# A hybrid decoder trunk on one core: the first stage in a written order with four column groups, the convolution's shifted copies by DMA, and a bias added as matrix products

## The chip, the cores and the metric

The kernel runs on one core of one Trainium2 chip. The core has five engines with instruction streams of their own: TensorE (PE, with its weight loads shown apart as PEld), VectorE (DVE), ScalarE (ACT), GpSimd (POOL) and SyncE (SP). Sixteen DMA engines move data between the chip's memory and the core's SBUF. The metric is the device time of one execution in microseconds (us).

## The reference

Two layers over 256 tokens with D = 2048 features, all in float32. Layer 0 mixes tokens with a Conformer convolution module, layer 1 with differential attention; each is followed by an MLP with 8192 hidden units. Every sublayer is modulated by vectors computed from one condition vector c (adaLN). What matters here is layer 0:

```python
cond = silu(c)
mod = cond @ ada_w[i] + ada_b[i]                # 2048 x 12288 weights per layer
sh_m, sc_m, g_m, sh_f, sc_f, g_f = split(mod, 6)
h = x * (1.0 + sc_m) + sh_m
# conformer_conv
u = h @ w1 + b1                                 # pw1: 2048 x 4096
a, gt = split(u, 2)
u = a * sigmoid(gt)
u = causal_depthwise_conv(u, w_dw, width=31) + b_dw
u = silu(layer_norm(u, g, b))
y = u @ w2 + b2                                 # pw2: 2048 x 2048
x = layer_norm(ALPHA * x + g_m * y)
h = x * (1.0 + sc_f) + sh_f                     # then the MLP, gated by g_f
```

## The kernel before

**Products.** TensorE multiplies in a fast 32-bit format with a rounded mantissa, so each float32 operand is split into a high and a low part. ACT casts a weight tile to the high part (`CAST wh...`, line 424), DVE subtracts it from the original (`wl...`, line 426), and each 128x128 by 128x512 step takes three products: high times high (L440), high times low weights (L441), low times high (L442). The 256 tokens are two row tiles t = 0, 1. KC = 16 chunks of 128 features are summed. pw1 is cut into eight column groups j of 256 value and 256 gate columns; a group of 16 chunks is 16 x 2 x 3 = 96 products in two PSUM banks. A weight tile of 4 chunks is 1 MB, loaded by two DMAs of 512 KB on SP's queue (L417) into one of four `wraw` buffers.

**Modulation vectors.** Each of the six vectors of a layer needs 16 MB of `ada_w`, read as 1 MB tiles `aw` (L206). DVE can do a tile: multiply by cond and add into `aacc` (L236), followed at the end by products with ones that sum over partitions (`apt`, L218). Or TensorE can: `aps` products with cond as 32 columns, eight per tile (L268), a copy by ACT to a row (L272), and transposes back (L253). In the first stage ada tiles and weight tiles share the four `wraw` buffers, and two `araw` buffers serve ada tiles alone.

**First stage.** `SLICES` cuts the 16 chunks into four slices of four. For each slice SC_M comes by DVE, SH_M by TensorE; h is formed transposed (`h_t`, split into `h_hi` and `h_lo`); and three groups of pw1, `FIRST = (2, 0, 1)`, add the slice's products. They stay open in PSUM over the four slices. The order on all engines is left to the scheduler of the tile framework. The stage ends with the last slice's products, at 188 us.

**Groups 3 to 7 and the convolution.** Then TensorE's order is as written. Each of the other five groups runs through its 16 chunks (`group`). `tick()` after every second chunk runs steps that were deferred with `defer(n, step)`. A finished group is copied from PSUM (`utok`, L760), transposed (L773, L774), and gated by ACT and DVE to u (L781, L783). The convolution (`conv_pe`) is done by TensorE on 32 features at a time: the 31 taps are eight products of four shifts each. For that u is laid out in four shifted copies, by 16 copies of 32 partitions per group, 12 by ACT (L729) and 4 by DVE (L731); then 64 products with 32 columns for each of two 128-feature halves (L738). Tap matrices are made by DVE (`conv_w`, L720).

**Other ada tiles.** G_M, SC_F and SH_F are needed later: `pump_conv` issues them beside the groups, `fill` in the tail behind the last group, `pump_t2` the rest during pw2. SH_F is done by TensorE, the others by DVE. By the start of pw2 42 of these 48 tiles are issued.

**Gate and bias.** `gate_and_base` (at tick 28) spreads the gate G_M to all partitions through two dependent DMAs (`gb_d`, `gb`), and `base_bias` loads the bias of pw2, multiplies it by the gate and adds it to z, all on POOL (L659, L663). pw2 runs from 420.6 us on in four column groups (L526 to L528); the gated result is added to z by DVE.

Of the kernel before, what the change touches and what calls it, by code (L numbers as in the profile page):

```python
# [19 lines left out]
P = 128  # L20
# [10 lines left out]
FIRST = (2, 0, 1)  # L31
ADA_T1 = 32
# [17 lines left out]
CV_AT = (1, 4)  # L50
OV_AT = (2, 4)
# [5 lines left out]
MAN_AT = None  # L57
SC_PE = ()
SLICES = ((0, 4), (4, 4), (8, 4), (12, 4))
SHIFT = ("act", "act", "act", "dve")  # L60
SHIFT_END = ("act", "dve", "act", "dve")
CONV_AT = {2: 1, 0: 4, 1: 7}
PE_WAIT = (3, 4)
# [16 lines left out]
def trunk(  # L80
# [114 lines left out]
    n_raw = [0]  # L195

# [13 lines left out]
    def ada_slice_dve_steps(i, v, f0, nf, m, first=True):  # L210
# [14 lines left out]
        def step(a):  # L225
            wv = load(a)
# [11 lines left out]
            if kc == KC - 1:  # L238
                if first:
                    finish()  # L240
                else:
                    defer(DVE_WAIT, finish)
        return [lambda a=a: step(a) for a in range(KC // per)]

    def ada_slice_steps(i, v, f0, nf, m, first=False, apart=False):
# [16 lines left out]
        def step(a):  # L262
            wv = st.pop(a, None) or load(a)
# [6 lines left out]
            if kc == KC - 1:  # L270
                st["rows"] = work.tile([P, NG], F32, tag="A", name=f"arow_{i}_{v}_{f0}")[:, :w]
                nc.scalar.copy(st["rows"], st["ps"])  # L272
                if first:
                    finish()
                else:
                    defer(2, finish)
        steps = [lambda a=a: step(a) for a in range(KC // per)]
        if apart:
            return [lambda a=a: st.update({a: load(a)}) for a in range(KC // per)], steps
# [41 lines left out]
    ada_q = []  # L321
    m_gm, m_scf, m_shf = mod_tile(0, G_M), mod_tile(0, SC_F), mod_tile(0, SH_F)
    for f0 in (0, 8):
        ada_q.extend(ada_slice_dve_steps(0, G_M, f0, 8, m_gm, False))
# [15 lines left out]
    n_late = 7 * KC  # L340

    def pump_early(n):
        for _ in range(n):
            if len(ada_q) > n_late:
                ada_q.pop(0)()
# [24 lines left out]
    def to_featT(src, pair, mul, add, name, c2s=None):  # L370

        for c2 in (range(KC // 2) if c2s is None else c2s):
            pt = tp_tile(f"{name}_t{c2}")
            for j in range(2):
                cc = 2 * c2 + j
                for t in range(NT):
                    nc.tensor.transpose(out=pt[:, j * S + t * P: j * S + (t + 1) * P],
                                        in_=src[:, t, cc * P:(cc + 1) * P], identity=ident)
            h32 = work.tile([P, 2, S], F32, tag="B", name=f"{name}_h{c2}")
            for j in range(2):  # L380
                cc = 2 * c2 + j
                if j == 0:
                    nc.vector.tensor_scalar(h32[:, j, :], pt[:, j * S:(j + 1) * S],
                                            mul[:, cc:cc + 1], add[:, cc:cc + 1], ALU.mult, ALU.add)
                else:
                    nc.scalar.activation(h32[:, j, :], pt[:, j * S:(j + 1) * S], AF.Identity,
                                         scale=mul[:, cc:cc + 1], bias=add[:, cc:cc + 1])
            put_split(pair, 2 * c2, 2, 0, S, h32)
# [24 lines left out]
    def load_split(src, name, on_pool=()):  # L413
        raw = wraw.tile([P, 2048], F32, tag="raw", name=f"w_{name}")[:, :src.shape[1] * NG]
        rv = raw.rearrange("p (a h n) -> p a h n", a=src.shape[1], h=src.shape[2])
        for h in range(src.shape[2]):
            raws["dma"] = nc.sync.dma_start(rv[:, :, h, :], src[:, :, h, :])  # L417
        parts = []
        per = 1024 // NG
        for q in range(src.shape[1] // per):  # L420
# [4 lines left out]
            eng = nc.gpsimd if q in on_pool else nc.vector  # L425
            eng.tensor_tensor(lo, rq, hi.bitcast(F32), op=ALU.subtract)  # L426
# [5 lines left out]
    def mm_parts(pss, pair, parts, kc0, nk):  # L432

        hi, lo = pair
        for a, (wh, wl) in enumerate(parts):
            kc = kc0 + a
            for t in range(NT):
                xh = hi[:, kc, t * P:(t + 1) * P]
                xl = lo[:, kc, t * P:(t + 1) * P]
                nc.tensor.matmul(pss[t], lhsT=xh, rhs=wh, start=(kc == 0), stop=False)  # L440
                nc.tensor.matmul(pss[t], lhsT=xh, rhs=wl, start=False, stop=False)  # L441
                nc.tensor.matmul(pss[t], lhsT=xl, rhs=wh, start=False, stop=(kc == nk - 1))  # L442
            if a % 2:
                tick()

    def group(pair, srcs, name, pump, on_pool=()):
# [4 lines left out]
        for i, src in enumerate(srcs):  # L451
            parts = load_split(src, f"{name}_{i}", on_pool)
            pump()
            mm_parts(pss, pair, parts, kc, nk)
# [8 lines left out]
    def add_group(key, pair, srcs, lead=False, tail=False, pump=None, start=None, pre_t=None, on_t=None,  # L463
                  only=None, prep=None, between=None, on_pool=()):
# [6 lines left out]
        for blk in blocks:  # L471
            if only is not None and blk[0] not in only:
# [3 lines left out]
                             start=start if first else None, pre_t=pre_t if first else None, pre_done=False, prep=prep if first else None, on_t=on_t,  # L476
# [25 lines left out]
    def run_jobs():  # L502
        banks, h = {}, 0
        for n, job in enumerate(jobs):
# [9 lines left out]
            def half(j, t):  # L514
# [3 lines left out]
                for a, (wh, wl) in enumerate(split[h + j]):  # L518
                    kc = kc0 + a
                    for tt in t:  # L520
# [5 lines left out]
                        nc.tensor.matmul(pss[tt], lhsT=xh, rhs=wh, start=(kc == 0), stop=False)  # L526
# [165 lines left out]
    XW = UW - 3  # L692
    ux = big.tile([P, 4096], F32, tag="uTh", name="conv_ux")
    xs_buf = [ux[:, 0:8 * XW], econv.tile([P, 8 * XW], F32, name="conv_x")]
    xs_buf = [x_.rearrange("p (n b s) -> p n b s", n=2, b=4) for x_ in xs_buf]
    u_buf = [ux[:, 8 * XW + i * 2 * UW:8 * XW + (i + 1) * 2 * UW].rearrange("p (n s) -> p n s", n=2) for i in range(3)]
# [15 lines left out]
    def conv_pe(j, u):  # L712


        xs = xs_buf[1 if j not in FIRST else FIRST.index(j) % 2]
        dg = [[], []]
# [8 lines left out]
        for b in range(4):  # L725
            for r in range(4):
                dst, src = xs[32 * r:32 * r + 32, :, b, :], u[32 * b:32 * b + 32, :, r:r + XW]
                if (SHIFT_END if j == 7 else SHIFT)[(r - b) % 4] == "act":
                    nc.scalar.copy(dst, src)  # L729
                else:  # L730
                    nc.vector.tensor_copy(dst, src)  # L731

        def products(n):
            ch = 2 * j + n
            ps = tp_tile(f"cv_{ch}")
            for k4 in range(8):
                for b in range(4):
                    nc.tensor.matmul(ps[32 * b:32 * b + 32, :S], lhsT=dg[n][k4 // 4][:, (k4 % 4) * 4 + b, :],  # L738
                                     rhs=xs[:, n, b, 4 * k4:4 * k4 + S],
                                     start=(k4 == 0), stop=(k4 == 7))  # L740
            dst = work.tile([P, S], F32, tag="S", name=f"vpe_{ch}", bufs=3)
            nc.scalar.activation(dst, ps[:, :S], AF.Identity, bias=cv["dwb"][:, ch:ch + 1])
            conv_done(ch, dst)
        return products

    n_conv = [0]
    n_early = len(ada_q) - n_late

    def pump_conv():
        n_conv[0] += 1  # L750
        while n_early - (len(ada_q) - n_late) < ADA_T1 * n_conv[0] / (4 * (8 - len(FIRST))):
            pump_early(1)

    conv_last = []

    def glu(j, pss, wait=1):
        ut = []
        for t in range(NT):
            u_t = work.tile([P, NG], F32, tag="A", name=f"utok_{j}_{t}")
            nc.scalar.copy(u_t, pss[t])  # L760
            ut.append(u_t)
        if j in FIRST:
            u = u_buf[FIRST.index(j)]
        else:
            u = work.tile([P, 2, UW], F32, tag="X", name=f"u_{j}", bufs=3)

        def rest():
# [630 lines left out]
```

## Time and profile before

| | us |
|---|---|
| median of 3 runs | 2434.58 (2431.07 to 2436.49) |
| profiled execution | 2432.41 |
| its span | 2430.6 |
| first stage ends (last product of the first three groups) | 188 |
| last product of pw1 | 386 |
| start of pw2 | 420.6 |
| first 128x512 products of the MLP's part behind pw2's | from about 514 on |

The span is the time between the first and the last instruction of the profiled execution; 1.8 us lie around it. The remaining 1900 us are the first MLP, the attention layer and the second MLP. In the profile's rows a name such as `L440 PE MATMUL pw_ps<-wh_pw,h_hi` reads: line 440 of the kernel, on PE, written tile, then the tiles read. A waits row names the waiting engine and tile, what ended the wait, then us in total, times, and the longest one.

### The profile page before, as it was taken

The numbers are of one execution on the slowest core, as the hardware profiler recorded it, in microseconds if no ns is written. First come the engines' busy times: TensorE is split into PE (matmuls) and PEld (weight loads), VectorE is DVE, ScalarE is ACT, GpSimd is POOL, SyncE is SP. The second block draws the span as 40 slices with busy tenths as digits, with TensorE's granted clock in tenths as the row PEclk, the third lists the DMA queues.
The fourth block names the chain that finished last, engine by engine and source line by source line (L and its number), as shares of the span: only waits on it lengthen the run. The fifth ranks groups of instructions, "written<-read, shape, count | busy, mean of one in ns | idle before, by whom it ended". The sixth has DMA issues, their size and how long they took to land.

```text
span 2430.6 us, 28467 instructions
## 1 busy us (share of the span) xinstructions
PE 2277.4 (94%) x11119; PEld 1816.0 (75%) x11119; DVE 1759.5 (72%) x1977; ACT 1070.6 (44%) x1391; POOL 264.9 (11%) x174
## 2 busy tenths in 40 slices
PE   4588997989999999999998999998999999999997
PEld 2366664867778888888876888886788888888886
DVE  5588744879798888878868777886867565565566
ACT  2337554444434434434444544443543443443442
POOL 0000011232150000000024200012214000000002
PEclk9789998999999999999999999999999999999999
DMA  9998767658988888888875666685676555556562
GB/s 354 312 331 292 247 220 263 240 209 290 333 309 319 293 322 278 315 314 294 299 254 189 203 237 220 236 291 185 236 277 227 190 186 190 191 185 197 181 223 102
DMA packets 272547, 609.57 MB, mean 251 GB/s; under 512 B 11098, under 2 KB 44448, under 8 KB 259100
## 3 DMA queue, kind: packets, MB, share of 16 engines
q1 hardware_dynamic: 271560, 607.24, 72.2%
q8 instruction: 87, 1.43, 0.2%
q10 hardware_dynamic: 852, 0.51, 0.1%
q14 instruction: 48, 0.39, 0.0%
HBM read 605.58 MB, written 2.13 MB: 250 GB/s over the span
## 4 chain that ended last, share of the span: by engine, by line
PE 75%; DVE 10%; DMA 6%; ACT 4%; issue 3%; POOL 1%; ACTq 0%; DVEq 0%; SPq 0%; POOLq 0%
PE w_ps L527 17%; PE w_ps L526 17%; PE w_ps L528 17%; DMA aw<-in_ada_w_dram 4%; DVE wl_w L494 2%; DVE aacc L236 2%; PE aps L268 1%; PE pw_ps L440 1%; DVE acc L294 1%; PE pw_ps L441 1%; PE qkv_q_ps L528 1%; PE pw_ps L442 1%; PE qkv_v_ps L528 1%; PE qkv_v_ps L526 1%; PE qkv_v_ps L527 1%
## 5 line engine op out<-in xcount | busy, mean ns | idle before, releaser
L494 DVE TENSOR_TENSOR wl_w<-w_w,wh_w 128x1024 fp32r<-128x1024 f32 x502 | 634.3, 1281 | 332.7 <-ACT wh_w L493 332.5
L493 ACT CAST wh_w<-w_w 128x1024 fp32r<-128x1024 f32 x512 | 537.5, 1053 | 754.1 <-PE w_ps L528 579.3
L526 PE MATMUL w_ps<-wh_w,hm_hi 128*128 128x512 f32 x1024 | 403.9, 394 | 4.5 <-ACT hm_hi L361 4.5
L527 PE MATMUL w_ps<-wl_w,u_hi 128*128 128x512 f32 x1024 | 399.0, 390 | 6.3 <-DVE wl_w L494 6.3
L527 PE MATMUL w_ps<-wl_w,hm_hi 128*128 128x512 f32 x1024 | 400.5, 391 | 4.7 <-DVE wl_w L494 4.7
L528 PE MATMUL w_ps<-wh_w,hm_lo 128*128 128x512 f32 x1024 | 400.8, 391 | 1.0 <-DVE hm_lo L364 1.0
L526 PE MATMUL w_ps<-wh_w,u_hi 128*128 128x512 f32 x1024 | 400.0, 391 | 0.0
L528 PE MATMUL w_ps<-wh_w,u_lo 128*128 128x512 f32 x1024 | 398.6, 389 | 0.0
L294 DVE SCALAR_TENSOR_TENSOR acc<-adaw,cond,acc 128x2048 f32<-128x2048 f32 (+1 forms) x105 | 243.0, 2315 | 0.1
L526 PEld LDWEIGHTS w_ps<-wh_w,hm_hi 128*128 128x128 f32 x1024 | 193.2, 189 | 49.2 <-ACT hm_hi L361 6.2
L527 PEld LDWEIGHTS w_ps<-wl_w,u_hi 128*128 128x128 f32 x1024 | 192.3, 188 | 47.9 <-DVE wl_w L494 8.4
L527 PEld LDWEIGHTS w_ps<-wl_w,hm_hi 128*128 128x128 f32 x1024 | 193.5, 189 | 45.1 <-DVE wl_w L494 6.0
L528 PEld LDWEIGHTS w_ps<-wh_w,hm_lo 128*128 128x128 f32 x1024 | 193.2, 189 | 43.0 <-DVE hm_lo L364 2.6
L526 PEld LDWEIGHTS w_ps<-wh_w,u_hi 128*128 128x128 f32 x1024 | 192.3, 188 | 42.0 <-issue 2.5
L528 PEld LDWEIGHTS w_ps<-wh_w,u_lo 128*128 128x128 f32 x1024 | 192.2, 188 | 39.9
L494 POOL TENSOR_TENSOR wl_w<-w_w,wh_w 128x1024 fp32r<-128x1024 f32 x10 | 24.0, 2404 | 1095.7 <-ACT wh_w L493 1095.7
L236 DVE SCALAR_TENSOR_TENSOR aacc<-aw,cond,aacc 128x512 f32<-128x512 f32 (+1 forms) x120 | 128.2, 1069 | 16.0 <-DMA aw<-in_ada_w_dram 14.0
L426 DVE TENSOR_TENSOR wl_pw<-w_pw,wh_pw 128x1024 fp32r<-128x1024 f32 x64 | 79.8, 1260 | 60.5 <-ACT wh_pw L424 60.4
L440 PE MATMUL pw_ps<-wh_pw,h_hi 128*128 128x512 f32 x256 | 106.6, 416 | 6.2 <-ACT h_hi L361 6.2
L441 PE MATMUL pw_ps<-wl_pw,h_hi 128*128 128x512 f32 x256 | 102.7, 401 | 0.0
L442 PE MATMUL pw_ps<-wh_pw,h_lo 128*128 128x512 f32 x256 | 99.1, 396 | 0.0
L424 ACT CAST wh_pw<-w_pw 128x1024 fp32r<-128x1024 f32 x64 | 65.9, 1048 | 68.6 <-PE pw_ps L442 58.7
(322 smaller groups left out, 3189.4 us busy)
## 6 DMA issues: line engine op xcount, KB each, us to landing
w_w<-in_mlp_w_dram SPq DMA_DIRECT2D x256, 1024.0 KB, 5.5
adaw<-in_ada_w_dram SPq DMA_DIRECT2D x96, 1024.0 KB, 6.1
aw<-in_ada_w_dram SPq DMA_DIRECT2D x84, 1024.0 KB, 7.3
w_pw<-in_conv_pw_w_dram SPq DMA_DIRECT2D x64, 512.0 KB, 7.2
w_pw<-in_conv_pw_w_dram SPq DMA_DIRECT2D x16, 1024.0 KB, 5.2
w_qkv_q<-in_attn_qkv_w_dram SPq DMA_DIRECT2D x16, 1024.0 KB, 5.3
w_qkv_k<-in_attn_qkv_w_dram SPq DMA_DIRECT2D x16, 1024.0 KB, 5.1
w_qkv_v<-in_attn_qkv_w_dram SPq DMA_DIRECT2D x16, 1024.0 KB, 5.2
```

What stands on the lines that cost most here:

```text
L236: nc.vector.scalar_tensor_tensor(st["acc"], wv[:, kc % per, :], cond[:, kc:kc + 1], st["acc"], ALU.mult, ALU.add)
L294: nc.vector.scalar_tensor_tensor(st["acc"], w, cond[:, kc:kc + 1], st["acc"], ALU.mult, ALU.add)
L424: nc.scalar.copy(hi, rq)
L426: eng.tensor_tensor(lo, rq, hi.bitcast(F32), op=ALU.subtract)
L440: nc.tensor.matmul(pss[t], lhsT=xh, rhs=wh, start=(kc == 0), stop=False)
L441: nc.tensor.matmul(pss[t], lhsT=xh, rhs=wl, start=False, stop=False)
L442: nc.tensor.matmul(pss[t], lhsT=xl, rhs=wh, start=False, stop=(kc == nk - 1))
L493: nc.scalar.copy(hi, rq)
L494: eng.tensor_tensor(lo, rq, hi.bitcast(F32), op=ALU.subtract)
L526: nc.tensor.matmul(pss[tt], lhsT=xh, rhs=wh, start=(kc == 0), stop=False)
L527: nc.tensor.matmul(pss[tt], lhsT=xh, rhs=wl, start=False, stop=False)
L528: nc.tensor.matmul(pss[tt], lhsT=xl, rhs=wh, start=False, stop=(kc == nk - 1))
```

## The change

1. **First stage.** The slices become (0,2), (2,4), (6,4), (10,4), (14,2), as first chunk and count. Four groups take part instead of three: `RES = (0, 1)` stay in PSUM; `ROT = (2, 3)` are closed after each slice and summed in SBUF, by an ACT copy for the first slice and a DVE addition for the others, in parts of `vtok`. PE, DVE, ACT and SP follow the order written in the code. Ada tiles no longer share `wraw`: they use two `araw` buffers and two halves of the tile `ux` (`conv_ux`), so four ada and four weight tiles can be in flight. The end of a slice's modulation (`end_ada`) stands in the middle of the previous slice's last group. The loads of `other_vectors` (nine small ones on ACT's queue) stand behind slice 2.
2. **Convolution.** `conv_pe` is cut into `conv_shift`, `conv_taps` and `conv_products`, placed at ticks `CONV_AT`. The shifted copies of groups 0 to 6 become 16 DMAs each on ACT's queue, of 32 partitions x 571 floats (73 KB); group 7 keeps copies, 8 by ACT and 8 by DVE. Two 128-feature halves are one copy with the padding between them.
3. **Ada tiles.** There are two queues: `dve_q` (16 tiles of G_M, 8 of SC_F) and `pe_q` (16 of SH_F, and 8 of SC_F that DVE did before). Twenty `dve_q` tiles run beside groups 4 to 7, eight `pe_q` tiles in the tail, and the remaining 16 of `pe_q` and 4 of `dve_q` during pw2.
4. **Bias and gate.** The bias of pw2 is added by two products (high and low part) that open each PSUM bank, with a one-row selector as stationary operand: 16 products. `base_bias` is not called for this layer any more. The gate's broadcast moves from tick 28 to the tail, behind the last convolution products.
5. The copies that fill `wct` are fewer and larger.

```diff
-FIRST = (2, 0, 1)
-ADA_T1 = 32
+RES = (0, 1)
+ROT = (2, 3)
+SLICES = ((0, 2), (2, 4), (6, 4), (10, 4), (14, 2))
+ADA_T1 = 20
-CONV_AT = {2: 1, 0: 4, 1: 7}
+CONV_AT = (3, 7, 11, 15, 19, 23, 28)
...
     def ada_raw(name, first):
-        n_raw[0] += 1
-        if first and n_raw[0] % 3:
-            return wraw.tile([P, 2048], F32, tag="raw", name=name)
+        if first:
+            n_raw[0] += 1
+            if n_raw[0] % 4 in (3, 0):
+                return ux[:, n_raw[0] % 4 // 3 * 2048:(n_raw[0] % 4 // 3 + 1) * 2048]
         return araw.tile([P, 2048], F32, tag="araw", name=name)
...
-    ada_q.extend(ada_slice_dve_steps(0, SC_F, 0, 8, m_scf, False))
+    dve_q.extend(ada_slice_dve_steps(0, SC_F, 0, 8, m_scf, False))
     for f0 in range(0, KC, 4):
-        ada_q.extend(ada_slice_steps(0, SH_F, f0, 4, m_shf))
-    ada_q.extend(ada_slice_dve_steps(0, SC_F, 8, 8, m_scf, False))
+        pe_q.extend(ada_slice_steps(0, SH_F, f0, 4, m_shf))
+    for f0 in range(8, KC, 4):
+        pe_q.extend(ada_slice_steps(0, SC_F, f0, 4, m_scf))
...
+    def conv_shift(j):
+        u = cs[j]["u"].rearrange("p n s -> p (n s)")
+        for b in range(4):
+            for r in range(4):
+                dst, src = xs_buf[j % 2][32 * r:32 * r + 32, b, :XW], u[32 * b:32 * b + 32, r:r + XW]
+                if j < 7:
+                    nc.scalar.dma_start(dst, src)
+                elif (r - b) % 2:
+                    nc.vector.tensor_copy(dst, src)
+                else:
+                    nc.scalar.copy(dst, src)
...
     for s, (f0, nf) in enumerate(SLICES):
         last = f0 + nf == KC
+        nxt = [] if last else ada_step[s + 1]
+        for n, g in enumerate(order[s]):
+            split_w()
+            pss = pss0[g] if g in RES else [tp_tile(f"pw1_{g}_{s}_ps{t}") for t in range(NT)]
+            k0, k1 = (0, KC - 1) if g in RES else (f0, f0 + nf - 1)
+            parts = w_parts.pop(0)
+            if n == len(order[s]) - 1 and not last:
+                mm_parts(pss, hT, parts[:nf // 2], f0, k0, k1, False)
+                end_ada(s + 1)
+                mm_parts(pss, hT, parts[nf // 2:], f0 + nf // 2, k0, k1, False)
+            else:
+                mm_parts(pss, hT, parts, f0, k0, k1, False)
+                for _ in range(2 if n == 0 and len(nxt) > 2 else 1):
+                    if nxt:
+                        ada_pair(s + 1)
+            if g in ROT:
+                for t in range(NT):
+                    if s == 0:
+                        nc.scalar.copy(accs[g][t], pss[t])
+                    else:
+                        nc.vector.tensor_tensor(accs[g][t], accs[g][t], pss[t], op=ALU.add)
+                cs[g]["ut"] = accs[g]
+            elif last:
+                glu_copy(g, pss)
+            if last and n in (1, 2):
+                glu(RES[n - 1])
+                conv_shift(RES[n - 1])
...
-        base_bias(gate0["gb"], conv_pw2_b[0], "base0", 2)
...
+                        if kc == 0 and job["bias"] is not None:
+                            for n, (sel, row) in enumerate(job["bias"]()):
+                                nc.tensor.matmul(pss[tt], lhsT=sel, rhs=row, start=(n == 0), stop=False)
...
+    conv_products(7, 1)
+    need((0, G_M))
+    gate0["gb"] = gate_bcast(mods[(0, G_M)], "gb0")
```

The order fences below list instructions in the order in which an engine issues them, with the line, the operation, the tile written, the tiles read, the shape, and a count where several alike follow each other.

SP's queue at the start of the program, before (aw is an ada tile with the number of its vector, 0 for SH_M and 1 for SC_M, then first chunk and part; z holds x; w_pw is a weight tile with group and part):

```order
1 L127 DMA rows_c<-in_c_dram 16x128
2 L206 DMA aw_1_0_0_141<-in_ada_w_dram 128x4x512
3 L206 DMA aw_1_0_1_148<-in_ada_w_dram 128x4x512
4 L206 DMA aw_1_0_2_154<-in_ada_w_dram 128x4x512
5 L206 DMA aw_1_0_3_164<-in_ada_w_dram 128x4x512
6 L866 DMA z<-in_x_dram 128x2048
7 L206 DMA aw_0_0_0_177<-in_ada_w_dram 128x4x512
8 L866 DMA z<-in_x_dram 128x2048
9 L206 DMA aw_0_0_1_185<-in_ada_w_dram 128x4x512
10 L206 DMA aw_0_0_2_191<-in_ada_w_dram 128x4x512
11 L206 DMA aw_0_0_3_197<-in_ada_w_dram 128x4x512
12 L206 DMA aw_1_4_0_338<-in_ada_w_dram 128x4x512
```

And in the changed program:

```order
2 L205 DMA aw_1_0_0_141<-in_ada_w_dram 128x8x256
3 L205 DMA aw_0_0_0_143<-in_ada_w_dram 128x8x256
4 L205 DMA conv_ux<-in_ada_w_dram 128x8x256 x2
5 L897 DMA z<-in_x_dram 128x2048 x2
6 L425 DMA w_pw_2_0_149<-in_conv_pw_w_dram 128x2x256 x2
7 L425 DMA w_pw_0_0_152<-in_conv_pw_w_dram 128x2x256 x2
8 L425 DMA w_pw_3_0_155<-in_conv_pw_w_dram 128x2x256 x2
9 L425 DMA w_pw_1_0_158<-in_conv_pw_w_dram 128x2x256 x2
10 L205 DMA aw_1_2_0_183<-in_ada_w_dram 128x4x512
11 L205 DMA aw_0_2_0_185<-in_ada_w_dram 128x4x512
12 L205 DMA conv_ux<-in_ada_w_dram 128x4x512 x2
13 L425 DMA w_pw_2_1_211<-in_conv_pw_w_dram 128x4x256 x2
```

The first slice now needs four ada tiles instead of eight, and weight tiles of all four groups stand ahead of the second slice's ada tiles.

ACT's order where a group's shifted copies are made, before (sg is the gate's sigmoid, conv_x the shifted copies, wh the cast weights of later chunks):

```order
119 L781 ACTIVATE sg_0_1538<-pg_1527,cols_conv 128x256
120 L781 ACTIVATE sg_1_1541<-pg_1527,cols_conv 128x256
121 L729 COPY conv_x<-u_1490 32x2x284 x12
122 L424 CAST wh_pw_4_2_1_1719<-w_pw_4_2_1712 128x1024
123 L424 CAST wh_pw_4_3_0_1841<-w_pw_4_3_1838 128x1024
```

And in the changed program, at the end of the first stage:

```order
92 L799 ACTIVATE sg_0_1171<-pg_1160,cols_conv 128x256
93 L799 ACTIVATE sg_1_1174<-pg_1160,cols_conv 128x256
94 L736 DMA conv_ux<-conv_ux 32x571 x16
95 L435 CAST wh_pw_3_4_0_1193<-w_pw_3_4_1040 128x1024
96 L435 CAST wh_pw_4_0_0_1279<-w_pw_4_0_1276 128x1024
97 L435 CAST wh_pw_4_0_1_1283<-w_pw_4_0_1276 128x1024
```

Sixteen DMA issues stand where twelve copies did, ahead of the casts of the next weight tiles.

TensorE's order where pw2 begins, before (swish is pw2's input, pw the PSUM bank of a row tile):

```order
948 L526 MATMUL pw_0_ps_3112<-wh_pw_0_0_0_3116,swish_hi 128x512
949 L527 MATMUL pw_0_ps_3112<-wl_pw_0_0_0_3117,swish_hi 128x512
950 L528 MATMUL pw_0_ps_3112<-wh_pw_0_0_0_3116,swish_lo 128x512
951 L526 MATMUL pw_0_ps_3113<-wh_pw_0_0_0_3116,swish_hi 128x512
952 L527 MATMUL pw_0_ps_3113<-wl_pw_0_0_0_3117,swish_hi 128x512
953 L528 MATMUL pw_0_ps_3113<-wh_pw_0_0_0_3116,swish_lo 128x512
```

And in the changed program (pw2b_hl is the split bias, one the selector):

```order
940 L538 MATMUL pw_0_ps_3026<-pw2b_hl,one_2668 128x512 x2
941 L539 MATMUL pw_0_ps_3026<-wh_pw_0_0_0_3030,swish_hi 128x512
942 L541 MATMUL pw_0_ps_3026<-wl_pw_0_0_0_3031,swish_hi 128x512
943 L542 MATMUL pw_0_ps_3026<-wh_pw_0_0_0_3030,swish_lo 128x512
944 L538 MATMUL pw_0_ps_3027<-pw2b_hl,one_2668 128x512 x2
945 L539 MATMUL pw_0_ps_3027<-wh_pw_0_0_0_3030,swish_hi 128x512
```

Two products for the bias open each of the eight banks of pw2; the aps products of 16 ada tiles (not shown here) follow later in this part.

More of the change, by code (lines that the diff above doesn't have):

```diff
@@ L237, in step @@
                                                    st["acc"], ALU.mult, ALU.add)
[L238 to L243, printed above, removed]
+            if kc == KC - 1 and not first:
+                defer(DVE_WAIT, finish)
+        steps = [lambda a=a: step(a) for a in range(KC // per)]
+        if first:
+            return [lambda a=a: st.update({a: load(a)}) for a in range(KC // per)], steps, finish
+        return steps
     def ada_slice_steps(i, v, f0, nf, m, first=False, apart=False):
@@ L960, in ln_t, with out_proj @@
         return [stats, norm]
[L962 removed]
+    def out_proj(pair, w2d, gate, name, pump, at_end, start=None, hold=False, on_pool=((),) * 4, bias=None):
         st = stats_tile(name)
```

379 lines of the change are left out of this document (206 added, 173 removed).

## Prediction, made before the changed kernel was run

> **What bounds the kernel now.** I read the page first: the engine shares and the chain that ended last.
>
> ```profile
> span 2430.6 us, 28467 instructions
> PE 2277.4 (94%) x11119; PEld 1816.0 (75%) x11119; DVE 1759.5 (72%) x1977; ACT 1070.6 (44%) x1391; POOL 264.9 (11%) x174
> PE 75%; DVE 10%; DMA 6%; ACT 4%; issue 3%; POOL 1%; ACTq 0%; DVEq 0%; SPq 0%; POOLq 0%
> ```
>
> TensorE bounds the whole, but the diff touches only the first 515 us, so I cut these into stages by the windows view (columns: stretch, length, then busy us of each engine with instructions in brackets, granted clock, DMA share, GB/s).
>
> ```profile
> 30.00:60.00 30.00, 21.48 (x86) 14.46 (x83) 17.21 (x23) 9.56 (x13) 0.00 (x0) 0.89 1.06 372
> 60.00:95.00 35.00, 13.14 (x80) 6.00 (x79) 23.33 (x54) 10.45 (x34) 0.00 (x0) 0.70 1.04 364
> 95.00:130.00 35.00, 26.62 (x115) 18.20 (x111) 19.35 (x33) 10.98 (x17) 0.00 (x0) 0.79 0.75 244
> 188.00:386.00 198.00, 186.42 (x1553) 130.69 (x1553) 130.16 (x176) 115.07 (x174) 17.48 (x12) 0.98 0.74 254
> 386.00:420.60 34.60, 23.66 (x224) 10.15 (x222) 11.59 (x29) 16.39 (x28) 0.72 (x1) 0.85 0.70 243
> 420.60:511.00 90.40, 88.10 (x397) 72.85 (x398) 72.14 (x67) 39.19 (x47) 20.91 (x7) 0.96 0.75 258
> ```
>
> Between 60 and 95 us TensorE works 13 of 35 us while transfers run full at 364 GB/s; between 95 and 130 us the transfers themselves fall to 244. From 188 us on TensorE is 94 to 97% busy (the tail from 386 to 420.6 excepted) and transfers have a quarter to spare. The first stage's waits of TensorE (us in total, times, longest):
>
> ```profile
> PE aps L268 <- DMA aw<-in_ada_w_dram: 27.0, 6, 11.4
> PE apt L218 <- DVE aacc L236: 14.4, 1, 14.4
> PE pw_ps L440 <- ACT h_hi L361: 6.2, 1, 6.2
> PE pa L773 <- ACT utok L760: 6.3, 1, 6.3
> ```
>
> So the first stage (to 188 us) is held by the 32 ada tiles of 1 MB. The timeline of TensorE gives the prices (start, us, what):
>
> ```profile
> 36.74 1.11 PE L253 MATMUL apt<-ident,arow 128*128 128x128 f32 x4 [0.71 <-ACT arow L272]
> 45.78 0.80 PE L440 MATMUL pw_ps<-wh_pw,h_hi 128*128 128x512 f32 x1 [6.22 <-ACT h_hi L361]
> 46.80 0.63 PE L440 MATMUL pw_ps<-wh_pw,h_hi 128*128 128x512 f32 x1
> 47.23 0.63 PE L441 MATMUL pw_ps<-wl_pw,h_hi 128*128 128x512 f32 x1
> ...
> 59.83 0.39 PE L442 MATMUL pw_ps<-wh_pw,h_lo 128*128 128x512 f32 x1
> ...
> 60.51 0.39 PE L442 MATMUL pw_ps<-wh_pw,h_lo 128*128 128x512 f32 x1
> ...
> 403.43 0.66 PE L253 MATMUL apt<-ident,arow 128*128 128x128 f32 x4
> ...
> 407.49 1.04 PE L268 MATMUL aps<-aw,condr 128*32 128x512 f32 x8
> ```
>
> A 128x512 product starts 0.68/3 = 0.227 us after the one before (59.83 to 60.51, three steps), and 0.43 us after it (46.80 to 47.23) just after a wait. An ada tile on TensorE costs 1.04 us.
>
> **The change, part by part.**
>
> *First stage.* Bytes of before up to 200 us:
>
> ```profile
> DMA packets 39848, 65.81 MB, mean 329 GB/s; under 512 B 1526, under 2 KB 20472, under 8 KB 39584
> aw<-in_ada_w_dram SPq DMA_DIRECT2D x43, 1024.0 KB, 8.7
> ```
>
> The stage needs 32 ada tiles (33.6 MB), x (2.1 MB), small vectors (0.5 MB) and half instead of three eighths of pw1 (16.8 instead of 12.6 MB): 52.9 MB. At the 364 GB/s of the window 60 to 95 this is 145 us. Before, 48.8 MB would have taken 134 us, but the stage ended at 188: 54 us were transfers not asked for in time. The written order keeps four ada and four weight tiles in flight. Per 4-chunk group step the transfers need 3.1 MB / 364 = 8.6 us; TensorE needs 24 x 0.227 + 1.04 = 6.5, at the slow step of 0.43 us it would be 11.4; DVE's rows:
>
> ```profile
> L236 DVE SCALAR_TENSOR_TENSOR aacc<-aw,cond,aacc 128x512 f32<-128x512 f32 x60 | 45.0, 750 | 5.1 <-DMA aw<-in_ada_w_dram 3.7
> L426 DVE TENSOR_TENSOR wl_pw<-w_pw,wh_pw 128x1024 fp32r<-128x1024 f32 x29 | 35.1, 1222 | 19.1 <-ACT wh_pw L424 19.0
> ```
>
> DVE needs 4 x 0.75 + 2 x 1.222 = 5.4 us, and about 1.2 for the new sums of ROT groups every second step. Transfers stay the bound. The last ada tile lands four 0.5 MB weight tiles (5.8 us) before the end, at about 140; then the chain from row transposes to first product, 36.74 to 45.78 = 9 us, and the last slice's products, 4 groups x 12 x 0.227 = 11: end at 160, against 188. Lower end 150 (the last products overlap the chain, no hole at the start), upper end 178 (below).
>
> Moved with it: the small loads on ACT's queue.
>
> ```profile
> 9.77 0.43 ACTq L127 DMA_DIRECT2D rows_ln<-in_ln_mix_b_dram  x1
> 20.55 0.32 ACTq L127 DMA_DIRECT2D rows_ln<-in_ln_ffn_g_dram  x1
> 20.90 0.43 ACTq L127 DMA_DIRECT2D rows_ln<-in_ln_ffn_b_dram  x1
> 23.24 0.32 ACTq L127 DMA_DIRECT2D rows_ln<-in_ln_mix_g_dram  x1
> 26.09 0.32 ACTq L127 DMA_DIRECT2D rows_ln<-in_ln_mix_b_dram  x1
> 26.44 1.28 ACT L905 ACT_TABLE_LOAD   x1 [16.78 <-DMA z<-in_x_dram]
> ```
>
> Six small loads took ACT from 9.8 to 26.4 us, 2.8 us each, since in the program's order transfers of SP and ACT share eight completion lanes, and one is issued only when the transfer eight before it has landed. Before, nobody needed ACT there. Now nine such loads stand behind slice 2, with the CASTs of slice 3 behind them: up to 9 x 2.8 = 25 us of ACT. Eight tiles in flight hold 8.4 MB = 23 us of transfers, which cover it; I take 0, and keep 10 for the range.
>
> *pw1 and convolution, 188 to 386.* The order fences show 16 DMAs where 12 ACT and 4 DVE copies stood. Rows of before in this window:
>
> ```profile
> L729 ACT COPY conv_x<-u 32x568 f32<-32x568 f32 x48 | 31.9, 664 | 8.0 <-DVE u L783 7.4
> L424 ACT CAST wh_pw<-w_pw 128x1024 fp32r<-128x1024 f32 x37 | 37.9, 1048 | 33.3 <-PE pw_ps L442 30.7 <-DMA aw<-in_ada_w_dram 2.4
> L440 PE MATMUL pw_ps<-wh_pw,h_hi 128*128 128x512 f32 x156 | 64.3, 412 | 0.0
> L268 PE MATMUL aps<-aw,condr 128*32 128x512 f32 x64 | 8.1, 601 | 1.5 <-DMA aw<-in_ada_w_dram 1.5
> L663 POOL TENSOR_TENSOR z<-z,base_b 128x512 f32<-128x512 f32 x8 | 11.9, 1511 | 0.3
> ```
>
> Four groups instead of five remain: 384 products instead of 3 x 156 = 468, so 84 x 0.227 = -19 us. The 8 ada tiles (64 aps rows) move behind: -8.3. The order's waits are those of before, one group's hand-over included (6.3 us). The shifts: per j 12 x 0.664 = 8.0 us of ACT go and 16 issues come, at 0.35 to 0.45 us each (rows above) 5.6 to 7.2 us if no lane is awaited, and 16 x 2.8 = 45 us if all are. Here transfers are at 0.74 of their time instead of 1.04, so lanes come free sooner; I take about 13 us a burst. Behind the burst on ACT stand CASTs, which run four buffers ahead, 4 x 2 x 6 x 0.227 = 10.9 us of products. So TensorE waits about 2 us in each of seven bursts: +14, less the 3 it waits for copies now. The window then lasts 198 - 19 - 8 + 11 = 182, a gain of 16 or 17. Ends: 0 and 45 - 11 = 34 us a burst.
>
> The Trainium skill (DMA: Bandwidth & Descriptors, Anatomy of one DMA) puts a transfer at 2.0 us + bytes/436e3, measured on GpSimd's path; 73 KB would be 2.2 us, and two rounds on eight lanes 4.4, which the products of four CASTs hide (rival 2). The same page (Rules for kernel authors) asks for 1 MB and 128 partitions per DMA; these have 32 partitions and 73 KB, which speaks against the change. No run here shows a transfer of this shape.
>
> *Tail, 386 to 420.6.* It keeps 8 ada tiles, and takes the gate broadcast (two dependent DMAs on SP) that ran hidden at 330 us.
>
> ```profile
> gb_d<-gb_r SPq DMA_DIRECT2D x1, 8.0 KB, 4.6
> base_b<-in_conv_pw_b_dram SPq DMA_DIRECT2D x4, 256.0 KB, 6.2
> ```
>
> SP is held one landing, 4.6 us, with ada tiles queued behind: +2, between 0 and 5.
>
> *pw2, 420.6 to 511.* 16 ada tiles come onto TensorE (8 of SH_F, 8 of SC_F that DVE did): 16 x 1.04 = 16.6; their transposes 4 x 0.66 = 2.6; the bias 16 x 0.227 = 3.6. Nothing hides these, since TensorE is 97% busy there. With 1 or 2 us of new waits for tiles: +24, between 20 and 32. Dropping POOL's bias work (L663 and its loads) gains 0: nothing waited for it.
>
> Sum, against the profiled 2432.4 (span 2430.6 and 1.8 around it): -28 - 16.5 + 2 + 24 = -18.5, so 2414. The median of the three runs, 2434.6, lies 2 us above the profiled one, less than their spread (2431.1 to 2436.5), so I leave the sum as it is. The MLPs and the attention are not touched.
>
> **The rivals.** Changes within 0.2%, 4.9 us, can't be told from none.
>
> 1. *ACT becomes the bound of the convolution (slower).* The small loads cost 2.8 us each, and 16 in a row are far more than ever stood there. SP's loads share the lanes, so SP too waits for shifts. If a burst holds ACT 22 us, TensorE waits 11 in each of seven, 77 instead of 14: 2414 + 63 = 2477; at 16 us a burst, 5 each, it is 2435. That, 16 us a burst, is where it decides. Against it: transfers have a quarter to spare.
> 2. *All hidden.* Landings are short, TensorE waits for no shift (-14), and the first stage ends at 152 (-8): 2392.
> 3. *The written order stalls (no gain).* In order, one late tile stops products, ada and splits together; at the slow step a group takes 11.4 us, over the transfers' 8.6. 20 steps at 2 us over 8.6 are lost against 160, with part caught up: end at 178, 2432. For it: clock 0.70 between 60 and 95 us, after two waits of over 10 us.
>
> The Trainium skill (TensorE: Matmul & The Clock Gate, Part 1: The HAM clock gate) halves the clock after about 3.4 us without work and restores it after as much work; the 0.43 us steps after the 6.2 us wait agree. By it, gaps of 8.6 - 6.5 = 2.1 us a group would leave the clock full, and only gaps gathered into one would bring rival 3.
>
> **How the numbers follow.** My forecast 0.40 (its own range 2402 to 2426), rival 1 0.20, rival 2 0.28, rival 3 0.12. The low end is rival 2 with the first stage at 150 and 2 us less elsewhere, 2382; the high end takes in rival 3 and rival 1 up to about 17 us a burst, 2445. Faster by over 0.2% takes the forecast, rival 2 and a third of rival 3: 0.72. Within 0.2%: 0.07, from rivals 3 and 1. Slower: 0.21.
>
> **What would show it.** First stage: its last pw1 product near 160 instead of 188, DMA share near 1 from 30 to 140, and few waits of aps for ada tiles. Shifts: seven bursts of 16 issues on ACT's queue, each about 13 us from first to last; CASTs of the next group behind them. pw2: the stage longer by some 24 us, with aps rows in it. It would be wrong if the bursts take over 16 us each, if SP's loads queue behind shifts so that DMA share in the window falls below 0.6, or if the first stage has holes in its DMA row.

## The result and the profile after

The changed kernel takes 2495.5 us (median, 2488.4 to 2497.4) against 2432.8 for the kernel before, run beside it: ratio 1.025, 95% interval 1.0226 to 1.0275, slower. The range ended at 2445. The page of the changed kernel (the same parts as before: span, engines, chain):

```profile
span 2494.2 us, 28690 instructions
PE 2310.3 (93%) x11223; PEld 1826.6 (73%) x11223; DVE 1730.0 (69%) x1945; ACT 1013.6 (41%) x1292; POOL 243.2 (10%) x162
PE 74%; DVE 9%; DMA 7%; issue 2%; ACT 2%; ACTq 1%; POOL 1%; SPq 0%; DVEq 0%; POOLq 0%
```

ACTq, the issuing of transfers on ACT, now stands on the chain with 1% of the span. Where the stages begin and end is read from the first and last start of a line's products (median duration, then first to last start), and from windows with the columns of the forecast's:

```profile
L452 PE MATMUL pw_ps<-wh_pw,h_lo x256: 387/393/632, 31.7 to 414.7; 128*128 128x512 f32 x128
L538 PE MATMUL pw_ps<-pw2b_hl,one x16: 392/491/791, 460.5 to 556.1; 4*128 4x512 f32 x16
L539 PE MATMUL w_ps<-wh_w,hm_hi x1024: 387/389/666, 596.0 to 2390.1; 128*128 128x512 f32 x171
```

```profile
60.00:95.00 35.00, 26.66 (x127) 18.49 (x126) 25.02 (x35) 12.70 (x17) 0.00 (x0) 0.95 1.07 373
95.00:130.00 35.00, 24.55 (x128) 16.81 (x130) 23.25 (x37) 16.42 (x27) 0.00 (x0) 0.93 0.80 280
130.00:165.00 35.00, 26.46 (x110) 19.28 (x103) 18.56 (x33) 8.94 (x12) 0.00 (x0) 0.77 0.76 243
199.50:415.00 215.50, 175.16 (x1409) 124.31 (x1409) 110.84 (x150) 55.65 (x86) 0.00 (x0) 0.87 0.66 202
415.00:460.50 45.50, 26.12 (x239) 9.96 (x238) 15.98 (x32) 18.71 (x32) 0.72 (x1) 0.80 0.72 255
```

pw1 ends at 415 instead of 386, pw2 starts at 460.5 instead of 420.6, and the MLP's first product comes at 596.0 instead of 531.4: all 64 us lie ahead of the MLP. (The table of times before gives about 514 for it; at 514 pw2's own products still run, up to 517.1.) To 95 us the written order does what the forecast held (TensorE 26.7 busy of 35 where it was 13.1, transfers at 373 GB/s). Then transfers fall to 280 and 243 GB/s. Between 95 and 165 us TensorE waits 8.5 us for an ada tile and 6.1 us for the rows of a small vector, and behind that, at 203.8, it waits for ACT. ACT's queue shows the bursts (start, length, issues) and what stood behind them:

```profile
200.59 15.46 ACTq L736 DMA_DIRECT2D conv_ux<-conv_ux  x16
216.09 3.89 ACT L435 CAST wh_pw<-w_pw 128x1024 fp32r<-128x1024 f32 x4 [16.08 <-DMA conv_ux<-conv_ux]
226.29 17.69 ACTq L736 DMA_DIRECT2D conv_x<-conv_ux  x16
...
277.08 0.84 ACT L799 ACTIVATE sg<-pg,cols_conv 128x256 f32<-128x256 f32 x2 [14.55 <-DMA conv_ux<-conv_ux]
```

```profile
218.14 0.79 PE L450 MATMUL pw_ps<-wh_pw,h_hi 128*128 128x512 f32 x1 [14.05 <-ACT wh_pw L435]
```

The first burst holds ACT for 15.5 us; the cast of group 3's last tile stands behind it, and TensorE waits 14.05 us for that cast. The seven bursts took 15.5, 17.7, 15.5, 11.4, 12.9, 11.6 and 10.1 us from first to last issue, 13.5 on average, where the forecast took 13. What each cost on TensorE was mis-sized. An issue that stands alone takes 0.52 us, above the 0.35 to 0.45 of the forecast, so 16 of them take over 8 us before any wait:

```profile
293.61 0.52 ACTq L736 DMA_DIRECT2D conv_x<-u  x1
```

In the first burst ACT also stands from 208.4 to 211.6 us before one issue, whose completion lane a 1 MB ada tile from SP's queue still holds.

### The profile page after: what moved, and what is told of

It reads as the page before. It is cut to its first block, busy times and chain, and to the rows that moved or that the text cites. A ratio compares the mean times of both kernels' runs of the same rounds, so it can differ in the third digit from the quotient of the medians.

```text
span 2494.2 us, 28690 instructions
## 1 busy us (share of the span) xinstructions
PE 2310.3 (93%) x11223; PEld 1826.6 (73%) x11223; DVE 1730.0 (69%) x1945; ACT 1013.6 (41%) x1292; POOL 243.2 (10%) x162
## 4 chain that ended last, share of the span: by engine, by line
PE 74%; DVE 9%; DMA 7%; issue 2%; ACT 2%; ACTq 1%; POOL 1%; SPq 0%; DVEq 0%; POOLq 0%
PE w_ps L539 17%; PE w_ps L542 17%; PE w_ps L541 17%; DMA aw<-in_ada_w_dram 3%; PE cv L758 2%; DVE wl_w L504 2%; DMA w_w<-in_mlp_w_dram 1%; PE aps L271 1%; PE pw_ps L539 1%; PE qkv_q_ps L542 1%; PE qkv_v_ps L542 1%; PE qkv_v_ps L539 1%; PE qkv_v_ps L541 1%; PE qkv_q_ps L541 1%; PE pw_ps L542 1%
## 5 line engine op out<-in xcount | busy, mean ns | idle before, releaser
L503 ACT CAST wh_w<-w_w 128x1024 fp32r<-128x1024 f32 x512 | 537.3, 1053 | 753.7 <-PE w_ps L542 586.8
L539 PE MATMUL w_ps<-wh_w,hm_hi 128*128 128x512 f32 x1024 | 403.3, 394 | 4.5 <-ACT hm_hi L363 4.5
L539 PE MATMUL w_ps<-wh_w,u_hi 128*128 128x512 f32 x1024 | 400.0, 391 | 0.0
L539 PEld LDWEIGHTS w_ps<-wh_w,hm_hi 128*128 128x128 f32 x1024 | 192.9, 188 | 49.4 <-ACT hm_hi L363 6.2
L541 PEld LDWEIGHTS w_ps<-wl_w,hm_hi 128*128 128x128 f32 x1024 | 193.1, 189 | 45.5 <-DVE wl_w L504 6.4
L539 PEld LDWEIGHTS w_ps<-wh_w,u_hi 128*128 128x128 f32 x1024 | 192.2, 188 | 42.1 <-issue 1.7
L450 PE MATMUL pw_ps<-wh_pw,h_hi 128*128 128x512 f32 x256 | 114.8, 449 | 25.6 <-ACT wh_pw L435 14.6
L451 PE MATMUL pw_ps<-wl_pw,h_hi 128*128 128x512 f32 x256 | 108.7, 425 | 6.2 <-DVE wl_pw L436 6.2
L452 PE MATMUL pw_ps<-wh_pw,h_lo 128*128 128x512 f32 x256 | 107.9, 422 | 0.0
L237 DVE SCALAR_TENSOR_TENSOR aacc<-aw,cond,aacc 128x1024 f32<-128x1024 f32 (+2 forms) x80 | 80.2, 1003 | 30.7 <-DMA aw<-in_ada_w_dram 29.0
L450 PEld LDWEIGHTS pw_ps<-wh_pw,h_hi 128*128 128x128 f32 x256 | 53.2, 208 | 54.4 <-ACT wh_pw L435 16.4
```

The source lines that it names most:

```text
L237: nc.vector.scalar_tensor_tensor(st["acc"], wv[:, kc % per, :], cond[:, kc:kc + 1], st["acc"], ALU.mult, ALU.add)
L450: nc.tensor.matmul(pss[t], lhsT=xh, rhs=wh, start=(kc == first), stop=False)
L503: nc.scalar.copy(hi, rq)
L539: nc.tensor.matmul(pss[tt], lhsT=xh, rhs=wh, start=(kc == 0 and job["bias"] is None), stop=False)
L541: nc.tensor.matmul(pss[tt], lhsT=xh, rhs=wl, start=False, stop=False)
```

## The experiments

Each run is compared with runs of the kernel before on the same chip (medians of these 2428.6 to 2431.3); intervals are 95%. S is the changed kernel with copies instead of shift DMAs, T is S with SC_F on DVE.

**The shifts by copies (S).**

```diff
-                if j < 7:
-                    nc.scalar.dma_start(dst, src)
-                elif (r - b) % 2:
+                if (r - b) % 4 == 3 if j < 7 else (r - b) % 2:
                     nc.vector.tensor_copy(dst, src)
```

> The changed kernel with the shifted copies of groups 0 to 6 made by 12 ACT and 4 DVE copies again; all else as changed (2495). Theory A, the shift DMAs hold ACT for 10 to 18 us a burst and the casts behind them starve TensorE: the stretch from the end of the first stage to the last pw1 product shrinks from 215 us by 20 to 35, total 2460 to 2475. Theory B, the written order and the moved ada tiles cost the time and the bursts mostly fall into slack: within 8 us of the changed kernel.

2460.3 us, ratio 1.0122 (1.0102 to 1.0142): 35 us gained by undoing one part (31 by the ratios, each to its own chip). pw1 ends at 377 instead of 415.

```profile
L452 PE MATMUL pw_ps<-wh_pw,h_lo x256: 387/392/632, 31.5 to 377.0; 128*128 128x512 f32 x128
200.00:377.00 177.00, 161.74 (x1398) 114.00 (x1399) 120.52 (x176) 109.44 (x165) 0.00 (x0) 0.95 0.58 196
```

Theory A holds. ACT works more (109 us of 177) and TensorE waits less: of the 38 us between this stretch and the 215.5 us of the changed kernel, 25 are idle time of TensorE, and 13 are longer busy time for nearly the same instructions, with a granted clock of 0.87 there and 0.95 here.

**The same part alone, in the kernel before.** The copies in `conv_pe` become `nc.scalar.dma_start(dst, src)` for j < 7.

> The kernel before with only the shifted copies of groups 0 to 6 issued as 16 DMAs on ACT's queue (two pieces of 284 columns per partition). Theory A: 20 to 40 us slower than before, 2453 to 2473. Theory B: within 8 us of before, since half of ACT's time is free there.

2473.9 us, 1.0178 (1.015 to 1.0207), 43 us slower, a little more than theory A said. TensorE's waits from 195 to 425 us in that run:

```profile
PE cv L740 <- DMA conv_x<-u: 21.6, 6, 7.0
PE pa L775 <- ACT utok L762: 12.0, 1, 12.0
```

Here the convolution's products wait for the transfers too, since they stand closer behind them.

**The shift DMAs on other queues.** `nc.gpsimd.dma_start` or `nc.sync.dma_start` in the changed kernel.

> The changed kernel with the 16 shift DMAs issued from POOL's queue instead of ACT's, so that no cast stands behind them. Theory A (ACT held): as good as copies, 2460 to 2475. If instead the landing of the transfers is what the convolution waits for, or SP's loads wait for lanes, it stays at 2485 to 2505.

> The changed kernel with the shift DMAs on SP's queue: ACT issues none, but they still share SP's eight completion lanes and stand ahead of weight and ada loads. If the cost was ACT held with casts behind it, this is about as good as copies or POOL's queue, 2455 to 2470. If the cost was SP's loads held by lanes and issues, it stays at 2480 to 2505.

2463.6 us (1.0129, 1.0108 to 1.0149) on POOL's queue and 2465.8 (1.0147, 1.0129 to 1.0164) on SP's, both nearly as good as copies. The transfers are the same, only ACT issues none. So the cost was ACT held, not the landing and not SP's loads sharing lanes. The Trainium skill (DMA: Bandwidth & Descriptors, Issuing engines are not separate DMA queues) says that issuing from another engine saves only the time to initiate the transfers, usually small. Here it was worth 30 us, since waits for lanes are part of that time and casts stand behind.

**Without the bias products.** The argument `bias` of pw2's `out_proj` is left out.

> The changed kernel without the 16 bias products of pw2 (the bias of pw2 is left out). Priced in the forecast at 16 x 0.227 = 3.6 us with nothing to hide them: 2491 to 2493. If they stood beside waits for tiles, no change within 2 us.

2485.6 us, 1.0226 (1.0202 to 1.025). From pw2's first L539 product to its last it takes 112.8 us instead of 120.1, 7.3 less, twice the forecast's 3.6, so both expectations miss. The timeline of the changed kernel shows a pair of bias products among the others:

```profile
497.32 0.40 PE L542 MATMUL pw_ps<-wh_pw,swish_lo 128*128 128x512 f32 x1
497.65 0.72 PE L538 MATMUL pw_ps<-pw2b_hl,one 4*128 4x512 f32 x2
498.30 0.51 PE L539 MATMUL pw_ps<-wh_pw,swish_hi 128*128 128x512 f32 x1
498.64 0.40 PE L541 MATMUL pw_ps<-wl_pw,swish_hi 128*128 128x512 f32 x1
```

From 497.32 to 498.64 are four steps, 1.32 us instead of 4 x 0.227 = 0.91. Without the pair it would be two steps, 0.45; the pair costs 0.87 us, and eight pairs 6.9. These products use 4 of 128 rows (`4*128`), and there is a gap before and behind them. The Trainium skill (TensorEngine Tiling (Array Packing), Key Properties) says that a change of the tiling mode drains TensorE. The gaps would fit that, but no run here shows whether a product with 4 rows counts as such a change.

**The bias on POOL again**, on T: `base_bias(gate0["gb"], conv_pw2_b[0], "base0", 2)` behind the gate's broadcast, no products.

> Shifted copies by ACT and DVE and SC_F on DVE (2447), and the bias of pw2 on POOL as before instead of 16 products. By the run without the bias, where pw2's stretch was 8 us shorter, 2437 to 2441. By the forecast's price of 16 x 0.227 us, 2443. If POOL's additions to z or the gate's late broadcast then hold the gated sums, 2450 or more.

2440.4 us (1.0043, 1.0028 to 1.0059) against T's 1.0069: pw2's stretch is 101.9 us instead of 109.7, 7.8 less. This agrees with no_bias.

**SC_F's upper tiles back on DVE (T).**

```diff
-    for f0 in range(8, KC, 4):
-        pe_q.extend(ada_slice_steps(0, SC_F, f0, 4, m_scf))
+    dve_q.extend(ada_slice_dve_steps(0, SC_F, 8, 8, m_scf, False))
...
```

The part left out gives the sum of these tiles a buffer of its own.

> On top of the shifted copies by ACT and DVE (2460): the upper 8 tiles of SC_F go back from TensorE to DVE, during pw2. The forecast's prices: 8 x 1.04 + 2 x 0.66 = 9.6 us off TensorE, which is over 95% busy there, so 2449 to 2453. Rival, DVE or the two tile buffers then hold pw2 (DVE 8 x 2.6 us more): no gain, 2457 to 2465.

2447.0 us, 1.0069 (1.0054 to 1.0084), 13 us less than S and 2 below the range. Unlike what was expected, the tiles did not run during pw2: `pump_conv` counts from 24 tiles and this queue has 32, so eight more ran on DVE beside groups 4 to 7 (42 instead of 25 of DVE's 128x1024 steps there). pw2's stretch fell from 118.4 to 109.7 us, and the tail from 45 to 38.

**The gate's broadcast from POOL's queue**, on S: the two DMAs of `gate_bcast` on `nc.gpsimd`.

> On top of the shifted copies by ACT and DVE (2460): the two DMAs that broadcast the gate are issued from POOL's queue, so that the ada loads behind them on SP don't wait for the gate's rows. If SP standing at the gate (4.5 us at 394 to 398.5 in that run) is what delays the tail's last tiles, the tail shrinks from 45 us by 4 to 6, total 2453 to 2457. If the tail is bound by two tile buffers alone, no change within 3.

2458.9 us (1.0115, 1.0098 to 1.0131): no change that can be told. The tail takes 43 us instead of 45. SP standing at the gate was not what set it; in S TensorE waits there 17.2 us for ada tiles in two buffers. What else delays them was not tried.

**Small vectors, casts and weight loads in the first stage.** The nine loads issued on POOL's queue at the start into tiles of their own (on S); then also `conv_vectors()` and `other_vectors()` called ahead of the first slice (on T):

> On top of the shifted copies by ACT and DVE (2460): the nine small loads behind slice 2 are issued on POOL's queue at the start into tiles of their own. If ACT held at 148.6 to 156 us and TensorE's 7 us of waits there set the end of the first stage, it ends 5 to 8 us earlier, total 2452 to 2455. If the transfers and the order make it up later, no change within 3.

> Shifted copies by ACT and DVE and SC_F on DVE (2447), and all small vectors are loaded and turned at the start of the program (the nine loads on POOL's queue), so that nothing but a slice's own end stands between slices. Theory C, ACT, DVE and TensorE held at slice ends stop SP's loads (holes in the transfers at 105 to 117 and 145 to 158 us): the holes shrink, the first stage ends 10 to 18 us earlier, 2430 to 2438. Theory D, transfers or another wait bound it anyway: 2443 to 2449.

2456.2 us (1.0101, 1.0086 to 1.0116) and 2443.8 (1.0057, 1.0037 to 1.0077): 4 and 3 us, no more than the intervals are wide. In the second, the holes are mostly gone (280 and 243 GB/s in the changed kernel):

```profile
95.00:130.00 35.00, 30.33 (x151) 21.41 (x150) 26.37 (x36) 11.90 (x15) 0.00 (x0) 0.95 1.03 356
130.00:165.00 35.00, 29.18 (x162) 21.89 (x161) 27.81 (x42) 13.13 (x17) 0.00 (x0) 0.98 0.94 308
```

So theory C names the holes rightly, and pw1 ends 8 us earlier than in T (373.5 instead of 381.6), but little of the gain arrives. In the profiled executions the MLP starts 6.4 us earlier than in T, and the part behind it, which no edit touches, takes 6 us longer; why isn't known.

`split_w()` for all four groups at the start of the last slice, and the first stage's weight loads on `nc.gpsimd` (both on T):

> Shifted copies by ACT and DVE and SC_F on DVE (2447), and the four casts of the last slice are all issued at its start, ahead of the shifted copies. If the 8 us that TensorE waits for group 3's cast behind the copies lies on the path, 2437 to 2441. If the casts of group 4 then stand behind the copies instead, 2444 to 2449.

> Shifted copies by ACT and DVE and SC_F on DVE (2447), and the first stage's weight loads are issued on POOL's queue, so that an ada load never stands behind a weight load that waits for its buffer. If the written order of SP (17 us at one weight load from 100 to 118, then 8 us of TensorE's wait for the ada tile behind it) sets the stage's end, 2433 to 2441. If the buffers come free no sooner, 2444 to 2450.

2448.9 us (1.0082, 1.0057 to 1.0106): no gain. Behind the copies now stand the next group's casts and the gate's sigmoid, for which TensorE waits 5.6 us instead of 6.0 for the cast. The loads on POOL's queue: 2461.7 us (1.0127, 1.0106 to 1.0149), 14 us slower, outside both expectations; transfers fall to 209 GB/s between 95 and 130 us. Why POOL's queue is worse was not pursued, so this run doesn't decide whether SP's written order holds the stage.

**What bounds the first stage.** Half of its ada tiles not loaded, and three groups instead of four, both on vectors_at_start:

> As vectors_at_start (2444), but in the first stage TensorE's vector SH_M is made from the tiles of SC_M, so that 16 of the 32 ada tiles (16.8 MB) are not loaded; instructions on TensorE, DVE and ACT are the same. If transfers bound the first stage, it ends up to 16.8 MB / 364 GB/s = 46 us earlier, limited by TensorE's and DVE's own work to some 25 to 35: total 2409 to 2419. If the waits in the written order on TensorE, ACT and DVE bound it, at most 10 us are gained: 2434 or more.

> As vectors_at_start (2444), but with three column groups in the first stage (ROT = (2,)) and five behind it, at convolution ticks (3, 7, 11, 15, 23, 31, 36). The forecast held that the fourth group costs the stage only its bytes (4.2 MB, 11.5 us) and saves 96 products (21.8 us) later: then 2452 to 2456. If the fourth group costs the stage its products in full, no change: 2442 to 2448.

2424.0 us (0.9974, 0.9964 to 0.9984), 20 us less: both expectations miss. Transfers were a bound, but close behind stand TensorE and DVE, busy 33.9 and 31.4 of 35 us between 60 and 95 us when half of the ada tiles aren't loaded:

```profile
60.00:95.00 35.00, 33.88 (x180) 23.50 (x178) 31.39 (x44) 14.35 (x18) 0.00 (x0) 1.00 0.84 282
95.00:130.00 35.00, 29.98 (x146) 21.40 (x145) 31.54 (x41) 12.01 (x15) 0.00 (x0) 0.90 0.91 308
```

Three groups took 2443.7 us (1.0055, 1.0035 to 1.0074), the same as four. By these times the fourth group in the first stage gains nothing: what is saved later is spent there. In the profiled executions the MLP starts 5 us earlier with four groups (537.3 against 542.3 us), half of the 10 us that the forecast's prices give; the totals don't show it.

**All together**: T, vectors at the start, bias on POOL, gate on POOL's queue.

> What was gained so far, together: shifted copies by ACT and DVE, SC_F on DVE, bias on POOL, gate broadcast from POOL's queue, all small vectors at the start. If the gains add (2495 - 35 - 13 - 7 - 3 - 1), 2434 to 2438, level with before; below 2427 it would beat it.

2431.7 us, 1.0004 (0.9992 to 1.0016), level with before and 2 us below the range. The gains add up to a little more than their sum, and the parts tried account for the whole loss. But the small vectors at the start are an edit that the kernel before doesn't have, and the next runs show what it is worth there.

**The one edit carried back to the kernel before.** `CV_AT = (0, 6)` with the change's larger copies; the larger copies alone; and the first with the nine loads on POOL's queue at the start.

> The kernel before (2431) with two edits: the convolution's vectors are turned in the first slice instead of the second, with the fewer, larger copies of the change. If ACT and DVE in alternation at 72 to 98 us are on the first stage's path there, 2422 to 2427; if the stage waits for ada tiles anyway, within 4 of before.

> The kernel before with only the fewer, larger copies of the convolution's vectors (16 instead of 64), in the second slice as before. If the chain of alternating copies at 72 to 98 us was the cost, nearly all of the gain of vectors_before (10 us): 2418 to 2422. If the place was, 2426 to 2431.

> As vectors_before (2419), and the nine small loads go on POOL's queue at the start into tiles of their own, so that TensorE no longer waits 8 + 2.7 us for the vectors made of them. If those waits are on the first stage's path, 2408 to 2414; if ada tiles set the pace, 2416 to 2421.

2418.8 us (0.9951, 0.9932 to 0.9969), 2431.1 (0.9997, 0.9987 to 1.0007) and 2411.4 (0.9917, 0.9904 to 0.9931). The first gains more than was expected (2422 at best). The larger copies do nothing by themselves; the gain comes with the place. The third beats both kernels by 20 us and 84 us. Its windows answer to those of before:

```profile
60.00:95.00 35.00, 31.83 (x167) 21.46 (x166) 25.42 (x36) 9.89 (x13) 0.00 (x0) 0.95 1.06 375
95.00:130.00 35.00, 30.96 (x144) 20.99 (x144) 24.41 (x40) 10.43 (x14) 0.00 (x0) 0.80 1.05 374
130.00:165.00 35.00, 25.68 (x112) 20.04 (x112) 26.09 (x32) 25.42 (x36) 0.00 (x0) 0.90 1.08 369
```

With vectors out of the way, the scheduler's order fills the transfers from 30 to 165 us (before: 244 GB/s between 95 and 130), and pw1 ends at 363 instead of 386. So, with the small vectors moved towards the start in both, what is left of the change (written order, four groups, four tiles in flight, other placement of ada tiles) is 20 us slower than the kernel before: 2431.7 against 2411.4.

## Why the prediction was wrong, point by point

By the forecast's steps pw2 should have started at 160 + 182 + 36.6 = 378.6 us; it started at 460.5, 82 us later. That is the whole miss (2414 against the profiled 2496). The last product of the first stage's four groups came at 225 instead of 160, which is 65 of the 82; pw1 behind it took 190 us instead of 182, and the tail 45.5 instead of 36.6.

- **First stage, forecast 160 us.** This step failed first and most. Group 3's last products began only at 218 and ended at 225. The price of transfers was right (373 GB/s to 95 us), but the sum of bytes was read as a time, and the end as one chain of 20 us behind it. The stage's last ada product came at 173, where the forecast had the last ada tile land at 140:

```profile
L271 PE MATMUL aps<-conv_ux,condr x80: 379/605/1061, 19.4 to 173.2; 128*32 128x512 f32 x48, 128*32 128x256 f32 x32
```

  Behind it the stage took 51 us instead of 20. In the written order 96 of the 384 products come after it (21.8 us at 0.227), where the forecast counted 48. Three more things were not in the forecast. First, at slice ends the vectors' work holds ACT, DVE and TensorE, with SP behind them:

```profile
100.55 17.08 SPq L425 DMA_DIRECT2D w_pw<-in_conv_pw_w_dram  x4
...
143.93 17.43 SPq L425 DMA_DIRECT2D w_pw<-in_conv_pw_w_dram  x4
...
148.58 0.32 ACTq L124 DMA_DIRECT2D rows_adab<-in_ada_b_dram  x1
...
155.60 0.40 ACTq L124 DMA_DIRECT2D rows_subg<-in_attn_subln_g_dram  x1
156.04 1.99 ACT L435 CAST wh_pw<-w_pw 128x1024 fp32r<-128x1024 f32 x2 [6.86 <-DMA rows_b<-in_mlp_b_dram]
```

  SP twice stands 17 us at weight loads whose buffers the late splits hold. The nine loads, costed at 0 because "eight tiles in flight" covered them, held ACT for 7 us, and their cover was not there: SP stood before full buffers, and transfers fell to 76 GB/s between 151 and 158 us.

  Second, the first burst delayed group 3 by 14 us. Third, the fourth group is not free: three_groups showed no difference in the total.

  Yet clearing all vectors gave only 3 us in the total. In vectors_at_start the last ada product comes at 152, 21 us earlier than in T, but the last product of the four groups only 8 us earlier (208 against 216), since more waits for splits and casts follow it. Which of these sets the end was not tried, so part of the excess over 160 stays without a cause. Rival 3 said that the written order stalls, but its end of 178 was far short too.
- **Shifts, forecast 2 us of TensorE a burst, +14.** The length of a burst was right (13.5 against 13), its cost was not: copies gave back 35 us, 5 a burst. "Casts run four buffers ahead" took four full buffers for granted; the bursts stand where the gate's sigmoid and casts are due, the first one with nothing cast ahead. Rival 1 named the mechanism, with its turning point at 5 us a burst. The 2.2 us worked out from the Trainium skill (DMA: Bandwidth & Descriptors, Anatomy of one DMA) come near the 2.1 us median landing of two of the later bursts, but the estimate of 4.4 us a burst did not come true:

```profile
conv_x<-u ACTq DMA_DIRECT2D x32, 71.4 KB, 2.1
conv_x<-conv_ux ACTq DMA_DIRECT2D x16, 71.4 KB, 7.7
```

  The transfers of the second burst land in 7.7 us, beside ada tiles. With eight lanes a burst of 16 needs every lane twice, so it pays for such a landing before its last issue.

  Of the three signs of being wrong, the third came: the first stage has holes in its DMA row (20 GB/s between 110 and 117 us). The bursts stayed below 16 us on average, and the DMA share of the window at 0.66.
- **Tail, forecast +2.** It became 45.5 us instead of 34.6. TensorE waits 19.1 us for ada tiles, 5.2 at the longest, where the kernel before waited 7.8; that is about the whole difference:

```profile
PE aps L271 <- DMA aw<-in_ada_w_dram: 19.1, 5, 5.2
```

  The gate was priced rightly as small (gate_on_pool); the term that was missing is that these tiles come later, and why they do is open.
- **pw2, forecast +24.** From its first product to the MLP's first: 135.5 instead of 110.8, so +24.7. Right as a sum; within it the bias was 7 us, not 3.6, and the waits for tiles that were added did not come (0.7 us).
- **POOL's bias at 0**: right in the sense that nothing waited for it; by the same token moving it to TensorE could only cost (6.6 us in bias_on_pool).

## What to carry to other kernels

Before putting transfers on the queue of an engine that also works, list what stands behind them on that engine; a burst of small transfers costs the engine the whole time to its last issue. Here the same transfers from POOL's or SP's queue took within 6 us of copies. In a stretch bound by transfers, first move one-off work (vectors, tables) out of it; here that alone beat the rewritten order with the same edit by 20 us. A cover of "tiles in flight" counts only if the buffers are not already full.

## What was not expected of the hardware

A product with 4 rows among products with 128 cost 0.87 us a pair where 0.45 would be its share, by gaps on both sides. Transfers ran at 373 to 375 GB/s over 35 us with 1 MB and 512 KB tiles in flight, and TensorE (33.9 of 35 us) and DVE (31.4) were the next bounds right behind them.
